# First product's right operand loaded in place of its low part; four more pairs begun early; last sums delayed

## The chip, the cores and the metric

The kernel runs on one core of a Trainium2 chip. The metric is device time of one execution in microseconds, the median over runs. Five engines run their own instruction queues in order: PE (TensorE) multiplies, DVE (VectorE) and ACT (ScalarE) do elementwise work and bring results out of PSUM, POOL (GpSimd) does a few small operations and issues some DMAs, SP (SyncE) issues most DMAs. An instruction that waits for a semaphore holds all behind it in its queue.

## The reference

One layer of a hybrid encoder over x of 2048 rows by 1024 columns, in float32:

```
y = rmsnorm(x); z = y @ w_in                 # 1024 x 2576
a = gmlp_mixer(zu, zv, ...)                  # spatial gating in blocks of 128 rows
b = gla_mixer(zq, zk, zv, zg, zlr, ...)      # gated linear attention, chunks of 64 rows
m = concat([a, b]) @ w_out
h = x + rmsnorm(m)
f = rmsnorm(h) @ w_ff1                       # 1024 x 4096
f = square(relu(f)) @ w_ff2                  # 4096 x 1024
out = h + rmsnorm(f)
```

Every float32 operand of a large product is split into a high part (rounded to the fast format) and a low part (the rest), and three products of parts are added (`mm3`, L143).

## The kernel before

The mixer works on four blocks of 512 rows (b = 0 to 3). For each it forms the columns of z in groups (`group`, L579): vb, q, k, g, then the previous block's out-projection (`out_proj`, L541), then v and u. Smaller work (attention, gating, norms, transposes) is put between the matmuls by a list of jobs, `Jobs`, one step or more after each of the eight k steps of a product. In this part PE's order is the written one, and a scheduler orders DVE, ACT, POOL and SP.

The first product of the feed-forward, f = rmsnorm(h) @ w_ff1, is done in two halves of 1024 rows (p = 0, 1) and 16 column groups (q), by Strassen's scheme in Winograd's form: seven block products p1 to p7, of which each takes one left operand (a block or sum of w1 blocks) and one right operand (a block or a sum of blocks of the transposed, normalised h). Step s is the pair (p, q), so steps 0 to 15 are the first half, 16 to 31 the second. One block product is one tick: 12 matmuls of 512 columns. The order of ticks is `seq` (L651): within a step p2, p6, p5, p7, then p1 of the next step, p4, p3. Products of chain A (p1, p6, p7, p4) add up in one PSUM bank, which ACT copies out in between: p7 may start only when p6 has been copied, p4 only when p7 has. Work on the other engines hangs on ticks by a table, `plan`, and after L648 the order of all engines is the written one.

The right operand has seven keys (`RIGHT`: b11, b21, t2, t1, t3, t4, b22) of four k each: 28 pairs of a high and a low tile of 128 x 512 for each half, numbered n = 0 to 27. Blocks come from `ht_d` in HBM, the transposed h; the sums t1 to t4 come from `b_d`, which `sums` (L499) fills for the first half during the last block's first groups: it reads blocks of `ht_d` into two tiles `hs`, takes four differences on DVE, and stores them. To make a pair, `read_ht` loads 256 KB into a staging tile `hr`, `split_ht` copies it to the high tile on ACT (the rounding) and subtracts the high tile from the staging tile on DVE, into the low one. For p = 0 `ahead` (L627) does this for 20 pairs during the last out-projection, with four staging tiles of tag "four"; pairs 20 to 27 are staged in the first four ticks, in tiles of the weights' staging tag. For p = 1 `ht_in` (L748) stages a pair in tiles of tags "four", "hts" or "w2s" one to three keys ahead of its tick in step 15, and `ht_split` makes it two ticks after the key's last use by step 15. The tags "four" and "w2s" also carry the second product's right operand on its way to HBM (`split_w2`, `read_w2`; tiles th, tl, w2s and the tensor t_d). High and low tiles take the 36 buffers of tag "big" that the mixer used, and for n = 10 to 19 the 20 buffers of the pool `fr`.

The second product runs after the first, with the right operand read back from t_d. In names of tiles in the profile hh and hl are the high and low part of the right operand, wh and wl of a weight or left operand, ws a weight's staging tile, abh and abl the parts of the mixer's output, zu, zvb the groups' outputs, u, ux, uy the results of a step, pp a group's or the out-projection's PSUM bank, pf the first product's.

Of the kernel before, what the change touches and what calls it, by code (L numbers as in the profile page):

```python
# [9 lines left out]
F32 = mybir.dt.float32  # L10
# [3 lines left out]
ALU = mybir.AluOpType  # L14
# [3 lines left out]
P = 128  # L18
D = 1024
# [11 lines left out]
NQ = 16  # L31
RP = 1024
NP = S // RP
H = RP // 2
# [9 lines left out]
FIRST = ("p1", "p2", "p6", "p5", "p7", "p4", "p3")  # L44
# [58 lines left out]
def trunk(  # L103
# [4 lines left out]
    v, a, pe, pool, dma = nc.vector, nc.scalar, nc.tensor, nc.gpsimd, nc.sync  # L108
# [5 lines left out]
    wp = ctx.enter_context(tc.tile_pool(name="wp", bufs=1, reuse_waits="tile"))  # L114
# [9 lines left out]
    ht_d = [dram.tile([P, KT, TB], F32, name=f"ht_d{b}") for b in range(NB)]  # L124
    f_d = [[dram.tile([P, 2, D], F32, name=f"f_d{p}_{q}") for q in range(NQ)] for p in range(NP)]
    b_d = [[dram.tile([P, 4, H], F32, name=f"b_d{p}_{k}") for k in range(4)] for p in range(NP)]
# [10 lines left out]
    def slot(name, dt=F32, tag="big"):  # L137
        return big.tile([P, 512], dt, name=name, tag=tag, bufs=4 if tag == "four" else NBIG)

    def split_lo(out_lo, src, hi):  # L140
        v.tensor_tensor(out_lo, src, hi.bitcast(F32), ALU.subtract)  # L141
# [9 lines left out]
    def rsqrt(small, ss, n, scale, name):  # L151
        r = small.tile([P, n], F32, name=f"rs_{name}", tag="rs", bufs=9)
        v.tensor_scalar(r, ss, scale, EPS, ALU.mult, ALU.add)
        pool.tensor_tensor(r, r, mhalf[:, :n], ALU.pow)
        return r
# [35 lines left out]
    def stage(name):  # L191
        return wp.tile([P, 512], F32, name=name, tag="ws", bufs=NS)
# [301 lines left out]
        eng.tensor_tensor(out_, x_, y_, ALU.add)  # L494

    def minus(eng, out_, x_, y_):
        eng.tensor_tensor(out_, x_, y_, ALU.subtract)

    def sums(p, k):  # L499


        bs_ = []
        for c in range(2):
            st = wp.tile([P, D], F32, name=f"hs{p}_{k}_{c}", tag="xr", bufs=4)
            for n in range(2):
                dma.dma_start(st[:, n * H:(n + 1) * H], ht_d[2 * p + n][:, k + 4 * c, :])
            bs_.append((st[:, 0:H], st[:, H:RP]))
        (b11, b12), (b21, b22) = bs_
        t1, t2 = (wp.tile([P, 512], F32, name=f"ht{n}_{p}_{k}", tag="hts", bufs=2) for n in (1, 2))
        yield 1  # L510
        minus(v, t1, b12, b11)
        minus(v, t2, b22, t1)
        minus(v, b12, b22, b12)
        minus(v, b21, b21, t2)
        for n, t in enumerate((t1, t2, b12, b21)):
            dma.dma_start(b_d[p][k][:, n, :], t)

    ht = {}
    PAIRS = [(key, k) for key in RIGHT for k in range(4)]

    def read_ht(p, n, st):

        key, k = PAIRS[n]
        if key[0] == "t":
            dma.dma_start(st, b_d[p][k][:, int(key[1]) - 1, :])
        else:
            dma.dma_start(st, ht_d[2 * p + int(key[2]) - 1][:, k + 4 * (int(key[1]) - 1), :])

    def split_ht(p, n, st):
        key, k = PAIRS[n]  # L530
        pair = []
        for part in "hl":
            if 10 <= n < 20:
                pair.append(fr.tile([P, H], F32R, name=f"h{part}{p}_{key}_{k}", tag="ht", bufs=20))
            else:
                pair.append(slot(f"h{part}{p}_{key}_{k}", F32R))
        hi, lo = ht[p, key, k] = pair
        a.copy(hi, st)
        split_lo(lo, st, hi)

    def out_proj(b, steps=2, also=None):  # L541
        def before(hf, k):
# [40 lines left out]
    for b in range(NB):  # L583
# [10 lines left out]
        if b == NB - 1:  # L594
            jobs.add(*((lambda k=k: sums(0, k), 1) for k in range(4)))
# [26 lines left out]
        finish(b, 3)  # L622
        jobs.add(*((lambda i=i: gate(i), 4) for i in tiles))
    fr = br = None
    begun_ht = []

    def ahead(hf, k):  # L627

        nonlocal fr, br
        if hf == 0 and k == 1:  # L630
            mixp.close()
            br = ctx.enter_context(tc.tile_pool(name="br", bufs=1, side="right", reuse_waits="tile"))
            fr = frp.enter_context(tc.tile_pool(name="fr", bufs=1, side="right", reuse_waits="tile"))
        for _ in range(2 if hf or k == 3 else int(1 <= k < 3)):
            if len(begun_ht) < 20:
                n = len(begun_ht)
                st = slot(f"hr0_{n}", tag="four")
                read_ht(0, n, st)
                split_ht(0, n, st)
                begun_ht.append(n)  # L640

    out_proj(NB - 1, 4, ahead)


# [9 lines left out]
    at = {sn: i for i, sn in enumerate(seq)}  # L654
    todo = {}

    def plan(tick, fn, *args):
        todo.setdefault(tick, []).append((fn, args))

    def do(tick):  # L660
        for fn, args in todo.pop(tick, ()):
            fn(*args)
# [54 lines left out]
    def norm_m():  # L717
        v.tensor_tensor(sh[:, 0, :], sh[:, 0, :], sh[:, 1, :], ALU.add)
        last_h["r"] = rsqrt(wp, sh[:, 0, :], TPB, 1.0 / D, "m_last")

    def residual(t):
        h, xr = last_h[t]
        v.scalar_tensor_tensor(h, h, last_h["r"][:, t:t + 1], xr, ALU.mult, ALU.add)
        dma.dma_start(h_d[NT - TPB + t], h)
        a.activation(xr, h, AF.Square, accum_out=sh[:, 2, t:t + 1])
# [17 lines left out]
        plan(tick, fn, *args)  # L743


    staged = {}

    def ht_in(p, n):  # L748
        if p == 0:
            st = stage(f"hr{p}_{n}")  # L750
        elif n % 12 < 4:
            st = slot(f"hr{p}_{n}", tag="four")
        elif n % 12 < 6:
            st = wp.tile([P, 512], F32, name=f"hr{p}_{n}", tag="hts", bufs=2)
        else:
            if n % 2 == 0:
                staged["two"] = br.tile([P, D], F32, name=f"hr{p}_{n}", tag="w2s", bufs=3)
            st = staged["two"][:, n % 2 * H:(n % 2 + 1) * H]
        staged[p, n] = st
        read_ht(p, n, st)  # L760

    def ht_split(p, n):
        split_ht(p, n, staged.pop((p, n)))

    for n in range(20, 28):
        plan((n - 20) // 2, ht_in, 0, n)
        plan((n - 20) // 2 + 1, ht_split, 0, n)
    for n in range(28):

        plan(at[NQ - 1, FIRST[n // 4 - 3]] + 2 if n >= 12 else at[NQ - 1, "p1"] + 1 + n // 8, ht_in, 1, n)  # L770
    for n in range(28):
        todo.setdefault(at[NQ - 1, FIRST[n // 4]] + 2, []).insert(n % 4, (ht_split, (1, n)))


    def sums_in(k):
# [218 lines left out]
        read_w1(1, n)  # L994
    for i in sorted(j for j in todo if j < 0):
        do(i)
    norm_m()
    residual(0)
    for i in range(len(seq)):
# [120 lines left out]
    for m, (p, c) in enumerate(chunks):  # L1120
        banks = {}
        final = m == NCH - 1
        for grp in ((0, 1), (2, 3)) if final else (range(NPAIR),):
            for n7, n in enumerate(SECOND):
                name, key, chain = WINO[n]
                j = 7 * m + n7
                if grp[0] == 0 and j + 2 < 7 * NCH:
                    read_t(j + 2)
                for r in grp:
# [4 lines left out]
                    for kk in range(2):  # L1134
                        hi, lo = left[m, name, kk]
# [83 lines left out]
```

## Time and profile before

| | |
|---|---|
| runs | 2060.32, 2061.06, 2061.36 us; median 2061.06 |
| profiled execution | 2057.67 us, of which its span is 2055.7 |
| PE busy | 1999.5 us (97%), 9504 matmuls |
| DVE busy | 1422.9 us (69%) |
| ACT busy | 979.5 us (48%) |
| DMA | 446.86 MB, mean 217 GB/s |
| mean granted clock of TensorE | 0.992 |

The profile is of one execution. "Idle before" is the time that an engine sat idle ahead of an instruction, with what released it. The granted clock is the share of TensorE's 2.4 GHz that it was given. The last out-projection runs from about 734 to 782 us, the first product from 782 to about 1420 us, and its change from the first to the second half of the rows lies around 1080 to 1125 us.

### The profile page before, as it was taken

How to read it: one execution, taken by the hardware profiler on the slowest of the kernel's cores; microseconds unless marked ns; L12 is line 12 of the kernel's file. 1: busy time of each engine (PE TensorE's matmuls, PEld its weight loads, DVE VectorE, ACT ScalarE, POOL GpSimd, SP SyncE). 2: the span in 40 equal slices, each digit the busy share in tenths (PEclk: the TensorE clock that was granted, in tenths of full speed). 3: DMA queues.
4: the chain of work that ended last, by engine and by line, in shares of the span. 5: the costliest groups of instructions: out<-in, count | busy, mean ns of one | idle time of the engine just before them, and what ended most of it. 6: DMA issues, size and time to landing. Idle time of an engine off the chain costs nothing.

```text
span 2055.7 us, 27515 instructions
## 1 busy us (share of the span) xinstructions
PE 1999.5 (97%) x9504; PEld 1654.6 (80%) x9504; DVE 1422.9 (69%) x2491; ACT 979.5 (48%) x1942; POOL 250.7 (12%) x410
## 2 busy tenths in 40 slices
PE   8999999999899998999998999999999999999996
PEld 6989887988788886888887788888888888788885
DVE  4474467356735775657677677775888888988877
ACT  5464465356344555556667666666221214222212
POOL 0010011002100200003321333231000002100011
PEclk9999999999999999999999999999999999999998
DMA  7434245424852554758888878888767677866674
GB/s 217 126 114 132 81 141 149 148 78 154 260 177 86 166 197 144 249 197 259 287 288 287 274 276 289 285 273 292 265 236 264 237 265 272 323 253 257 242 268 185
DMA packets 165212, 446.86 MB, mean 217 GB/s; under 512 B 23488, under 2 KB 48592, under 8 KB 151376
## 3 DMA queue, kind: packets, MB, share of 16 engines
q1 hardware_dynamic: 138464, 355.42, 51.7%
q0 software_dynamic: 26608, 89.67, 12.3%
q8 instruction: 75, 1.23, 0.2%
q14 instruction: 65, 0.53, 0.1%
HBM read 319.19 MB, written 125.83 MB: 216 GB/s over the span
## 4 chain that ended last, share of the span: by engine, by line
PE 75%; DMA 9%; DVE 6%; issue 4%; ACT 3%; POOL 2%; SPq 0%; POOLq 0%; DVEq 0%; ACTq 0%
PE po_A L144 5%; PE po_A L145 5%; PE po_A L146 5%; PE pf_A L144 5%; PE pf_A L146 5%; PE pf_A L145 4%; PE pp_o L144 3%; PE pp_o L146 3%; PE pp_o L145 3%; PE po_C L144 2%; PE po_C L145 2%; PE po_C L146 2%; PE pf_C L144 2%; PE pf_C L146 2%; PE pf_C L145 2%
## 5 line engine op out<-in xcount | busy, mean ns | idle before, releaser
L494 DVE TENSOR_TENSOR acc<-acc,po_A 128x512 f32<-128x512 f32 x232 | 159.3, 687 | 47.3 <-PE po_A L146 33.0
L950 ACT CAST sh_s<-r 128x512 fp32r<-128x512 f32 x96 | 55.6, 618 | 165.4 <-PE po_A L146 92.9
L950 ACT CAST sh_a<-f 128x512 fp32r<-128x512 f32 x94 | 54.6, 618 | 130.4 <-DMA f<-f_d 92.6
L144 PE MATMUL pf_A<-hl_t,wh_s 128*128 128x512 f32 x256 | 102.5, 400 | 10.6 <-ACT uy L895 6.9
L141 DVE TENSOR_TENSOR wl_s<-s,wh_s 128x512 fp32r<-128x512 f32 x96 | 66.1, 689 | 60.6 <-ACT wh_s L692 60.5
L144 PE MATMUL pp_o<-wl_o,abh 128*128 128x512 f32 x256 | 103.8, 406 | 2.3 <-DVE h L451 2.0
L144 PE MATMUL po_A<-tt,sh_s 128*128 128x512 f32 x256 | 100.7, 393 | 2.5 <-DVE acc L494 1.4
L219 DVE SCALAR_TENSOR_TENSOR wl_o<-ws_o,outg,wh_o 128x512 fp32r<-128x512 f32 x64 | 47.9, 749 | 78.7 <-ACT wh_o L218 78.5
L146 PE MATMUL pf_A<-hh_t,wl_s 128*128 128x512 f32 x256 | 101.4, 396 | 0.0
L145 PE MATMUL pf_A<-hh_t,wh_s 128*128 128x512 f32 x256 | 100.8, 394 | 0.0
L144 PE MATMUL po_C<-tt,sh_s 128*128 128x512 f32 x256 | 100.5, 392 | 0.3 <-DMA tt<-t_d_b 0.3
L146 PE MATMUL pp_o<-wh_o,abl 128*128 128x512 f32 x256 | 100.4, 392 | 0.0
L145 PE MATMUL pp_o<-wh_o,abh 128*128 128x512 f32 x256 | 100.4, 392 | 0.0
L145 PE MATMUL po_A<-tt,sh_s 128*128 128x512 f32 x256 | 100.3, 392 | 0.0
L145 PE MATMUL po_C<-tt,sh_s 128*128 128x512 f32 x256 | 100.2, 392 | 0.0
L146 PE MATMUL po_A<-tt,sl_s 128*128 128x512 f32 x256 | 99.9, 390 | 0.0
L146 PE MATMUL po_C<-tt,sl_s 128*128 128x512 f32 x256 | 99.9, 390 | 0.0
L144 PE MATMUL po_A<-tt,sh_a 128*128 128x512 f32 x248 | 97.5, 393 | 0.5 <-DMA tt<-t_d_t 0.5
L494 DVE TENSOR_TENSOR acc<-acc,po_C 128x512 f32<-128x512 f32 x120 | 82.5, 687 | 21.4 <-PE po_C L146 14.0
L145 PE MATMUL po_A<-tt,sh_a 128*128 128x512 f32 x248 | 97.1, 392 | 0.0
L146 PE MATMUL po_A<-tt,sl_a 128*128 128x512 f32 x248 | 96.8, 390 | 0.0
L141 DVE TENSOR_TENSOR wl_a<-w1s,wh_a 128x512 fp32r<-128x512 f32 x96 | 66.0, 687 | 41.9 <-ACT wh_a L692 41.9
(299 smaller groups left out, 5974.1 us busy)
## 6 DMA issues: line engine op xcount, KB each, us to landing
tt<-t_d_t SPq DMA_DIRECT2D x61, 1024.0 KB, 6.0
tt<-t_d_b SPq DMA_DIRECT2D x46, 1024.0 KB, 4.8
w1s<-in_w SPq DMA_DIRECT2D x64, 512.0 KB, 5.1
f<-f_d SPq DMA_DIRECT2D x64, 512.0 KB, 7.1
ws_o<-in_w_out SPq DMA_DIRECT2D x64, 256.0 KB, 2.6
w2s<-in_w POOLq DMA_DIRECT2D x32, 512.0 KB, 6.4
t_d_t<-th_t POOLq DMA_DIRECT2D x64, 256.0 KB, 5.0
t_d_t<-tl_t POOLq DMA_DIRECT2D x64, 256.0 KB, 4.7
```

Source lines behind the costliest of these rows:

```text
L141: v.tensor_tensor(out_lo, src, hi.bitcast(F32), ALU.subtract)
L144: pe.matmul(ps, ahi, blo, start=start, stop=False, **kw)
L145: pe.matmul(ps, ahi, bhi, start=False, stop=False, **kw)
L146: pe.matmul(ps, alo, bhi, start=False, stop=stop, **kw)
L219: v.scalar_tensor_tensor(lo, st, gain, hi.bitcast(F32), ALU.mult, ALU.subtract)
L494: eng.tensor_tensor(out_, x_, y_, ALU.add)
L950: a.copy(hi, src)
```

## The change

Three edits. First, `read_ht` now takes both tiles of a pair and loads the values straight into the low one; `split_ht` copies from there to the high tile and subtracts in place. No staging tile is left, and `ht_in`, `ht_split` and their staging go. For p = 1 a key is read right behind its last tick in step 15 and split three ticks later (before: staged earlier, split two ticks later). Second, `ahead` reads by a table and splits a call later what was read the call before; it reads 24 pairs (before: 20) in the out-projection. The last four are read before the first tick and split at ticks 2 and 3. Third, `sums` yields 5 in place of 1 between its reads and its differences, takes its two DVE tiles only then, and the first difference keeps its place in the written order. PE's and POOL's instructions stand in the same order as before.

```
     def sums(p, k):
...
         (b11, b12), (b21, b22) = bs_
+        yield 5
         t1, t2 = (wp.tile([P, 512], F32, name=f"ht{n}_{p}_{k}", tag="hts", bufs=2) for n in (1, 2))
-        yield 1
-        minus(v, t1, b12, b11)
+        tc.keep_in_program_order(minus(v, t1, b12, b11))
...
-    def read_ht(p, n, st):
...
-            dma.dma_start(st, b_d[p][k][:, int(key[1]) - 1, :])
-        else:
-            dma.dma_start(st, ht_d[2 * p + int(key[2]) - 1][:, k + 4 * (int(key[1]) - 1), :])
-
-    def split_ht(p, n, st):
+    def read_ht(p, n):
         key, k = PAIRS[n]
         pair = []
         for part in "hl":
...
-        hi, lo = ht[p, key, k] = pair
-        a.copy(hi, st)
-        split_lo(lo, st, hi)
+        ht[p, key, k] = pair
+        if key[0] == "t":
+            dma.dma_start(pair[1].bitcast(F32), b_d[p][k][:, int(key[1]) - 1, :])
+        else:
+            dma.dma_start(pair[1].bitcast(F32), ht_d[2 * p + int(key[2]) - 1][:, k + 4 * (int(key[1]) - 1), :])
+
+    def split_ht(p, n):
+        hi, lo = ht[(p,) + PAIRS[n]]
+        a.copy(hi, lo.bitcast(F32))
+        split_lo(lo, lo.bitcast(F32), hi)
...
     def ahead(hf, k):
...
-        for _ in range(2 if hf or k == 3 else int(1 <= k < 3)):
-            if len(begun_ht) < 20:
...
+        if hf == 0:
+            n = {1: 3, 2: 6, 3: 9}.get(k, 0)
+        else:
+            n = {4: 12, 5: 14, 6: 16, 7: 18, 0: 20, 1: 22, 2: 23, 3: 24}[k]
+        for j in range(begun_ht[1], begun_ht[0]):
+            split_ht(0, j)
+        begun_ht[1] = begun_ht[0]
+        for j in range(begun_ht[0], n):
+            read_ht(0, j)
+        begun_ht[0] = max(n, begun_ht[0])
...
+    for n in range(24, 28):
+        plan(n // 2 - 10, split_ht, 0, n)
+    for n in range(28):
+        plan(at[NQ - 1, FIRST[n // 4]], read_ht, 1, n)
+        todo.setdefault(at[NQ - 1, FIRST[n // 4]] + 3, []).insert(n % 4, (split_ht, (1, n)))
...
-    for n in range(20, 28):
-        plan((n - 20) // 2, ht_in, 0, n)
-        plan((n - 20) // 2 + 1, ht_split, 0, n)
-    for n in range(28):
-        plan(at[NQ - 1, FIRST[n // 4 - 3]] + 2 if n >= 12 else at[NQ - 1, "p1"] + 1 + n // 8, ht_in, 1, n)
-    for n in range(28):
-        todo.setdefault(at[NQ - 1, FIRST[n // 4]] + 2, []).insert(n % 4, (ht_split, (1, n)))
...
+    for n in range(begun_ht[1], 24):
+        split_ht(0, n)
+    for n in range(24, 28):
+        read_ht(0, n)
     norm_m()
```

SP's queue in the last block, where q's weights (ws_3_q) are loaded. b_d0 is the store of a difference, hs0 a read for the sums. Before:

```order
L516 DMA b_d0_1_130<-ht1_0_1_5930 128x512
L208 DMA ws_3_q_0_6008<-in_w_in 128x256
L516 DMA b_d0_1_130<-ht2_0_1_5931 128x512
L516 DMA b_d0_1_130<-hs0_1_0_5924 128x512
L516 DMA b_d0_1_130<-hs0_1_1_5927 128x512
L516 DMA b_d0_2_131<-ht1_0_2_5964 128x512
L208 DMA ws_3_q_0_6008<-in_w_in 128x16
L506 DMA hs0_3_0_6000<-ht_d0_93 128x512
L516 DMA b_d0_2_131<-ht2_0_2_5965 128x512
L516 DMA b_d0_2_131<-hs0_2_0_5958 128x512
L516 DMA b_d0_2_131<-hs0_2_1_5961 128x512
L506 DMA hs0_3_0_6000<-ht_d1_94 128x512
```

After, around the first store of a difference:

```order
L208 DMA ws_3_q_4_6054<-in_w_in 128x256
L208 DMA ws_3_q_4_6054<-in_w_in 128x16
L208 DMA ws_3_q_5_6073<-in_w_in 128x256
L208 DMA ws_3_q_5_6073<-in_w_in 128x16
L208 DMA ws_3_q_6_6092<-in_w_in 128x256
L208 DMA ws_3_q_6_6092<-in_w_in 128x16
L516 DMA b_d0_0_129<-ht1_0_0_6000 128x512
L516 DMA b_d0_0_129<-ht2_0_0_6001 128x512
L516 DMA b_d0_0_129<-hs0_0_0_5890 128x512
L516 DMA b_d0_0_129<-hs0_0_1_5893 128x512
```

The stores and reads of the sums stood among the first two weights of q; now they begin behind the seventh.

ACT's queue in the last out-projection, up to the first eviction of its first half (h12 from pp_o3_0_0). wh_o3 is a weight, hr0 a staged read. Before:

```order
L218 ACTIVATE wh_o3_1_7_8050<-ws_o3_1_7_8048,outg_198 128x512
L538 CAST hh0_b21_3_7984<-hr0_7_7982 128x512
L538 CAST hh0_t2_0_8008<-hr0_8_8006 128x512
L218 ACTIVATE wh_o3_1_0_8080<-ws_o3_1_0_8078,outg_198 128x512
L538 CAST hh0_t2_1_8014<-hr0_9_8012 128x512
L450 ACTIVATE h12_7929,ssm3_7930<-pp_o3_0_0_7692 128x512
```

After:

```order
L218 ACTIVATE wh_o3_1_7_8064<-ws_o3_1_7_8062,outg_198 128x512
L539 CAST hh0_t1_3_8031<-hl0_t1_3_8032 128x512
L539 CAST hh0_b11_3_7884<-hl0_b11_3_7885 128x512
L218 ACTIVATE wh_o3_1_0_8092<-ws_o3_1_0_8090,outg_198 128x512
L539 CAST hh0_b21_0_7887<-hl0_b21_0_7888 128x512
L539 CAST hh0_b21_1_7890<-hl0_b21_1_7891 128x512
L450 ACTIVATE h12_7944,ssm3_7945<-pp_o3_0_0_7692 128x512
```

The casts just ahead of the evictions were of b21's last pair and of the first two pairs of t2, and are now of t1, b11 and the first two of b21. Earlier in this queue two casts of t2 now stand ahead of weight wh_o3_1_4 and two of t1 around the last cast abh15, where no cast of the right operand stood before.

ACT's queue where the second half's right operand begins (hh1), in step 15. wh_15 and wh_16 are left operands, uy14, ux15 and uy15 results of steps, and the COPY takes p6 of step 15 out of its bank. Before:

```order
L692 CAST wh_15_s1_10892<-s1_15_10790 128x512
L538 CAST hh1_b11_0_10924<-hr1_0_10896 128x512
L538 CAST hh1_b11_1_10928<-hr1_1_10898 128x512
L538 CAST hh1_b11_2_10932<-hr1_2_10900 128x512
L538 CAST hh1_b11_3_10936<-hr1_3_10902 128x512
L692 CAST wh_15_s3_10940<-w1s15_1_10643 128x512
L857 ACTIVATE uy14_10687<-uy14_10687 128x512
L858 ACTIVATE uy14_10687<-uy14_10687 128x512
L692 CAST wh_16_a11_10977<-w1s16_0_10739 128x512
L857 ACTIVATE ux15_10863<-ux15_10863 128x512
L858 ACTIVATE ux15_10863<-ux15_10863 128x512
L895 COPY uy15_10864<-pf15_A_10850 128x512
```

After:

```order
L697 CAST wh_15_s1_10876<-s1_15_10762 128x512
L697 CAST wh_15_s3_10893<-w1s15_1_10615 128x512
L841 ACTIVATE uy14_10659<-uy14_10659 128x512
L842 ACTIVATE uy14_10659<-uy14_10659 128x512
L539 CAST hh1_b11_0_10843<-hl1_b11_0_10844 128x512
L539 CAST hh1_b11_1_10846<-hl1_b11_1_10847 128x512
L539 CAST hh1_b11_2_10849<-hl1_b11_2_10850 128x512
L539 CAST hh1_b11_3_10852<-hl1_b11_3_10853 128x512
L697 CAST wh_16_a11_10924<-w1s16_0_10711 128x512
L841 ACTIVATE ux15_10835<-ux15_10835 128x512
L842 ACTIVATE ux15_10835<-ux15_10835 128x512
L879 COPY uy15_10836<-pf15_A_10822 128x512
```

The four casts of b11 stood ahead of the squares of uy14; now they stand behind them, still ahead of the squares of ux15 and the copy.

## Rows read from the trace of the kernel before

**Rows 1.** The page's first part: span, TensorE.

```profile
span 2055.7 us, 27515 instructions
...
PE 1999.5 (97%) x9504; PEld 1654.6 (80%) x9504; DVE 1422.9 (69%) x2491; ACT 979.5 (48%) x1942; POOL 250.7 (12%) x410
```

**Rows 2.** Busy time by stretch: instructions in brackets, granted clock, DMA share, GB/s.

```profile
core 0: us, PE busy (x) PEld busy (x) DVE busy (x) ACT busy (x) POOL busy (x), PEclk, DMA share, GB/s
740.00:830.00 90.00, 81.66 (x358) 65.81 (x357) 58.86 (x92) 54.28 (x100) 2.41 (x3) 0.94 0.57 185
1080.00:1165.00 85.00, 77.99 (x332) 62.83 (x331) 63.35 (x103) 60.93 (x111) 16.19 (x30) 0.98 0.84 279
```

**Rows 3.** TensorE in order of time: start, length, idle before it, releaser.

```profile
540.67 0.50 PE L144 MATMUL pp_vb<-wl_vb,yh 128*128 128x512 f32 x1 [1.57 <-ACT zu L283]
...
566.31 0.39 PE L144 MATMUL pp_q<-wl_q,yh 128*128 128x272 f32 x1 [3.83 <-ACT zvb L283]
...
758.14 0.79 PE L144 MATMUL pp_o<-wl_o,abh 128*128 128x512 f32 x1 [2.05 <-DVE h L451]
...
797.86 0.50 PE L144 MATMUL pf_A<-hl_t,wh_s 128*128 128x512 f32 x1 [3.29 <-ACT u L895]
...
812.45 0.59 PE L144 MATMUL pf_C<-hl_b,wh_s 128*128 128x512 f32 x1 [2.26 <-DVE hl_b L141]
...
1096.72 0.51 PE L144 MATMUL pf_A<-hl_t,wh_s 128*128 128x512 f32 x1 [2.07 <-ACT uy L895]
...
1120.17 0.80 PE L144 MATMUL pf_A<-hl_t,wh_s 128*128 128x512 f32 x1 [3.60 <-ACT uy L895]
```

**Rows 4.** Stretches of the same length, behind a wait and later; columns as in rows 2.

```profile
758.10:761.50 3.40, 3.36 (x8) 2.68 (x9) 3.40 (x6) 2.47 (x7) 0.00 (x0) 0.50 0.63 234
762.00:765.40 3.40, 3.40 (x17) 2.78 (x16) 1.88 (x4) 1.75 (x3) 0.00 (x0) 1.00 0.49 132
```

**Rows 5.** SP's waits in 518 to 572 (total, times, longest), and ScalarE's timeline.

```profile
SPq L516 <- DVE ht L497: 9.5, 8, 2.2
...
563.67 0.42 ACT L215 CAST wh_q<-ws_q 128x272 fp32r<-128x272 f32 x1 [6.54 <-DMA ws_q<-in_w_in]
```

**Rows 6.** ScalarE's timeline: the square ahead of u's fourth eviction.

```profile
539.32 0.63 ACT L425 ACTIVATE zv<-zu 128x512 f32<-128x512 f32 x1 [1.47 <-DVE zu L423]
```

**Rows 7.** VectorE groups in 1040 to 1160, a difference written over its input.

```profile
L497 DVE TENSOR_TENSOR w1s<-w1s,w1s 128x512 f32<-128x512 f32 x6 | 4.1, 682 | 0.0
```

**Rows 8.** ScalarE's timeline around the last out-projection.

```profile
740.77 0.72 ACT L218 ACTIVATE wh_o<-ws_o,outg 128x512 fp32r<-128x512 f32 x1 [2.00 <-PE pp_o L146]
...
754.85 0.62 ACT L538 CAST hh_t<-hr 128x512 fp32r<-128x512 f32 x1 [1.43 <-DMA hr<-b_d]
...
794.93 1.20 ACT L538 CAST hh_t<-hr 128x512 fp32r<-128x512 f32 x2
...
811.06 1.26 ACT L538 CAST hh_b<-hr 128x512 fp32r<-128x512 f32 x2 [5.36 <-DMA hr<-ht_d]
```

**Rows 9.** Waits of SP (1055 to 1150) and ScalarE (1065 to 1150).

```profile
SPq L527 <- DMA t_d_t<-th_t: 8.0, 1, 8.0
...
ACT hh_b L538 <- DMA hr<-ht_d: 4.8, 4, 1.9
```

**Rows 10.** ScalarE's and VectorE's timelines in the change of row half.

```profile
1109.60 2.17 ACT L538 CAST hh_t<-hr 128x512 fp32r<-128x512 f32 x4
...
1110.24 2.49 DVE L141 TENSOR_TENSOR hl_t<-hr,hh_t 128x512 fp32r<-128x512 f32 x4
...
1114.57 0.63 ACT L857 ACTIVATE uy<-uy 128x512 f32<-128x512 f32 x1 [1.76 <-DVE uy L494]
```

**Rows 11.** DMA in 1078 to 1112 (40 slices); to landing of all reads of hr.

```profile
GB/s 400 130 0 67 299 255 5 260 287 169 304 215 217 130 214 328 152 304 313 287 349 289 328 362 398 328 253 318 417 405 446 400 405 417 390 402 395 386 388 390
...
hr<-b_d SPq DMA_DIRECT2D x16, 256.0 KB, 7.0
...
DMA to landing us min/median/max: 2.0/5.1/15.8
```

More of the change, by code (lines that the diff above doesn't have):

```diff
@@ L496, in minus @@
     def minus(eng, out_, x_, y_):
-        eng.tensor_tensor(out_, x_, y_, ALU.subtract)
+        return eng.tensor_tensor(out_, x_, y_, ALU.subtract)
     def sums(p, k):
@@ L519, in trunk @@
     PAIRS = [(key, k) for key in RIGHT for k in range(4)]
-    def read_ht(p, n, st):
-        key, k = PAIRS[n]
-        if key[0] == "t":
-            dma.dma_start(st, b_d[p][k][:, int(key[1]) - 1, :])
-        else:
-            dma.dma_start(st, ht_d[2 * p + int(key[2]) - 1][:, k + 4 * (int(key[1]) - 1), :])
-    def split_ht(p, n, st):
+    def read_ht(p, n):
         key, k = PAIRS[n]
@@ L624, in trunk @@
     fr = br = None
-    begun_ht = []
+    begun_ht = [0, 0]
     def ahead(hf, k):
@@ L633, in ahead @@
             fr = frp.enter_context(tc.tile_pool(name="fr", bufs=1, side="right", reuse_waits="tile"))
-        for _ in range(2 if hf or k == 3 else int(1 <= k < 3)):
-            if len(begun_ht) < 20:
[L636 to L640, printed above, removed]
+        if hf == 0:
[8 more added lines that the diff above has]
+        begun_ht[0] = max(n, begun_ht[0])
     out_proj(NB - 1, 4, ahead)
@@ L743, in trunk @@
         plan(tick, fn, *args)
-    staged = {}
[L748 to L763, printed above, removed]
-    for n in range(20, 28):
-        plan((n - 20) // 2, ht_in, 0, n)
-        plan((n - 20) // 2 + 1, ht_split, 0, n)
-    for n in range(28):
-        plan(at[NQ - 1, FIRST[n // 4 - 3]] + 2 if n >= 12 else at[NQ - 1, "p1"] + 1 + n // 8, ht_in, 1, n)
-    for n in range(28):
-        todo.setdefault(at[NQ - 1, FIRST[n // 4]] + 2, []).insert(n % 4, (ht_split, (1, n)))
+    for n in range(24, 28):
[3 more added lines that the diff above has]
+        todo.setdefault(at[NQ - 1, FIRST[n // 4]] + 3, []).insert(n % 4, (split_ht, (1, n)))
+    staged = {}
     def sums_in(k):
```

## The prediction

> **What bounds the kernel now.** I read the page's first part, the waits of TensorE in order of time, the queues behind each wait, and last the granted clock. TensorE is busy 1999.5 of 2055.7 us [rows 1], so it sets the time, and a change that leaves its matmuls alone, as this one does, can only move the 56 us in which it is idle and the stretches in which it runs slowly. Three stages hold much of that: PE is busy 81.66 of 90 us around the last out-projection and 77.99 of 85 us where the second half of the rows takes over [rows 2]; the third is the last block's vb and q groups. Their waits are seven [rows 3]: A, 1.57 before a vb matmul and 3.83 before q; B, 2.05 between the halves of the out-projection, 3.29 before (0, p7) and 2.26 before (0, p3); C, 2.07 and 3.60 before (15, p7) and (16, p7). Right behind five of them the granted clock is 0.50, the lower level (1.2 GHz), for about 3.4 us: the one behind 758.14 is shown, with 8 matmuls where the same length at full clock has 17 [rows 4]; the others stand behind 566.31, 797.86, 812.45 and 1120.17. Each costs half its length, 1.7 us. The 2.07 us wait at 1096.72 is followed by none. So the seven waits with their five slow stretches are 18.67 + 8.5 = 27.2 us, the most that this change can reach.
>
> **A: the delayed sums.** Before, q's weights wait in SP's queue behind stores of sums that DVE has not made yet: SP stood 9.5 us, eight times, for them, and ACT waited 6.54 us for a q weight with the eviction of vb behind it in its own queue [rows 5]. That eviction is what q waits for. In the new order seven q loads stand ahead of the first store. The three differences that came before the vb eviction on DVE are gone too; the square at 539.32, which had waited 1.47 us for DVE, stands ahead of the fourth eviction of u, which PE waits 1.57 us for [rows 6, 3]. I let both waits go, 1.57 + 3.83, with the slow stretch behind q, 1.7: **7.1 us**. What is late next: the sums now stand among the weights of q, k and g. Reading a buffer again waits for its store, and SP then holds the k weights. There are five staging buffers and six pairs of converted weights ahead of PE, so a hold of one store and one load hides; from below the gain is 0 (the wait moves to k), from above 7.1. I take 7.1, since the loads that PE needs first are all ahead.
>
> **B: reads into the low part, four more pairs early.** The 56 copies and 56 subtractions stay. Only the operand of the subtraction changes, to its own output, and the trace has such subtractions: 682 ns [rows 7], four in a row with a staged source 2.49 us [rows 10], so nothing is paid. What changes is who waits for a buffer. Before, a read waits for one of four staging buffers, and ACT, in order, waits for the read: 1.43 us just ahead of the evictions between the halves, and 5.36 us in the first ticks, with p3's operand [rows 8]. After, SP issues the reads as fast as PE and the mixer's pool leave buffers.
> Between the halves: wait 2.05, slow stretch 1.7. The casts ahead of the evictions are now of pairs whose reads SP issues without waiting for a staging buffer; a read lands after 2.0 to 15.8 us, median 5.1 [rows 11]. I leave 0.6 us of the wait and count 1.45 + 1.7 = **3.15**; bounds 0 and 3.75.
> Two casts now stand ahead of the out-projection's weight at 740.77, where ACT had been idle 2.00 us [rows 8], and two more near the last abh, which TensorE needs within 2 us. Two casts fit, their landing may not: cost **0.6**, bounds 0 and 3.1 (a median landing less that idle time).
> The wait of 3.29: ACT's chain of residual, square and scale stays, and only the two casts of 1.20 us at 794.93, ahead of the copy, go [rows 8]. **1.2**; the slow stretch stays (2.1 us of wait is left, and 2.05 was followed by one). Bounds 0 and 3.29 + 1.7.
> The wait of 2.26: its pairs are read at the end of the out-projection instead of two ticks before use, so it goes with its slow stretch: **3.96**, bounds 0 and 3.96.
> B is 3.15 - 0.6 + 1.2 + 3.96 = 7.7 us.
>
> **C: the second half's right operand.** The first wait comes from four staging buffers that were still being stored: SP stood 8.0 us for a store, the reads came late, and ACT idled 4.8 us for them with the copy of p6 behind [rows 9]. After, no staging buffer is needed, and the casts stand a tick later, behind the squares. The 2.07 goes. A read can start only when PE has used the low part for the last time, and is cast three ticks later, 8.5 us (seven ticks took 1120.17 - 3.60 - 1096.72 = 19.85 us [rows 3], 2.84 each); reads of sums landed after 7.0 us median there [rows 11]. That fits, barely.
> The second wait is work: between the copies of (15, p7) and (16, p6) ACT does 16 casts and 5 of weights at 0.54 (four in 2.17), four Relu and Square pairs at 1.26, and two copies, 0.5 each: 8.7 + 2.7 + 5.0 + 1.0 = 17.4 us [rows 10]. Without the first wait (15, p7) would start at 1094.65, its copy is due at 1097.5, and (16, p7) starts seven ticks later, at 1114.5: ACT is done at 1114.9, 0.4 late, and 1.76 more if it waits for DVE as it did [rows 10]. I allow 0.5 for the copy behind it. 5.67 becomes 2.7: **3.0**, and the slow stretch stays. Bounds: nothing (the wait goes to 5.67) and 5.67 + 1.7.
>
> **Sum.** 7.1 + 7.7 + 3.0 = 17.8 us. The profiled execution took 2057.67 us (its span and 2.0 around it), so it would take 2039.9; the median of the three runs stands 3.4 above it, and I forecast from that: 2061.06 - 17.8 = **2043.3**.
>
> **A rule that speaks against C.** In 1078 to 1112 the slices of DMA traffic run at 386 to 446 GB/s from 1102 on [rows 11]. The new order issues four groups of four reads in four successive ticks, 4.2 MB in 11.4 us, 370 GB/s, and weights and stores run beside them. The Trainium skill ("DMA: Bandwidth & Descriptors", Bandwidth) has HBM's share of one core bind at about 358 GB/s; by it these reads alone would take 11.7 us, an estimate, the later groups would land past their casts, and it would side with the slower rival below. The measured slices are above its figure, so I do not take it.
>
> **Rivals.**
> 1. The reads are late in the out-projection as well: ACT waits there as before and B gives nothing. For it: ACT is in order, and a landing can take 15.8 us [rows 11]. Against: SP issues the reads many places ahead. 2061.06 - 7.1 - 3.0 = 2051.0.
> 2. The sums only move the hold of SP to k or g: A gives nothing. For it: SP stood 9.5 us for them [rows 5], and the same stores are still in its queue. Against: more weights are ahead of them. 2061.06 - 10.7 = 2050.4. Both together with C at nothing are no change, 2061.
> 3. Slower: a read for the second half now lies between the last use of its buffer and its cast, where before it went to staging two groups earlier. If reads land later than 8.5 us, ACT waits in each of seven groups with the copies behind it, PE waits for ACT, and the next buffers come free later. Each us past 8.5 costs 7 us. A and B without C are 14.8, so it turns slower than before from 8.5 + 14.8 / 7 = 10.6 us; at 12 us it is 2061.06 - 14.8 + 24.5 = 2071. For it: 15.8 was seen, and 7.0 is the median of sums. Against: both are with eight and more reads at once, which the new order spreads.
> 4. All seven waits and slow stretches go: 2033.9. Against: C's ACT work alone does not fit.
>
> **Chances.** Forecast (10 to 25 us gained) 0.58, range 2036 to 2051; rival 4 or near it 0.05; rival 1 0.15; rival 2 0.07; no change 0.07; rival 3 0.08. About 0.2%, 4.1 us, can be told from no change. Faster 0.58 + 0.05 + 0.15 + 0.07 = 0.85, same 0.07, slower 0.08. The range reaches from rival 4 to beyond rivals 1 and 2: 2034 to 2056; what is left out is the two worse cases and a little at the fast end.
>
> **What would show it.** Right: no wait of PE before pp_q and pp_vb's fourth tile, ACT without a DMA wait ahead of the evictions at the middle of the out-projection, no wait before the first p3, one slow stretch there in place of three; in the second half's change-over no ACT wait for a read, and one PE wait of 2 to 3 us before (16, p7). Wrong: q's wait found again before pp_k or pp_g; ACT idle for reads of hl in the out-projection; casts of the second half that wait for DMA.

## The result, and the profile after

The changed kernel takes 2040.22 us (median of six runs, 2037.61 to 2044.24) where the kernel before takes 2060.31 (six runs beside it): a ratio of 0.9903, 95% interval 0.9891 to 0.9916. The forecast was 2043.3, with 2034 to 2056 as its range. The profiled execution's span is 2036.6 us.

The page's first part, as in [rows 1]: TensorE has the same 9504 matmuls and is busy 5.5 us less, mostly since three slow stretches, 1.7 us each, are gone.

```profile
span 2036.6 us, 27539 instructions
...
PE 1994.0 (98%) x9504; PEld 1651.4 (81%) x9504; DVE 1422.3 (70%) x2491; ACT 980.8 (48%) x1942; POOL 251.1 (12%) x410
```

Busy time over the same matmuls as in [rows 2] (columns as there). The first stretch is 6.6 us shorter than its 90, the second 5.2 shorter than its 85.

```profile
732.10:815.50 83.40, 78.71 (x359) 63.67 (x358) 58.75 (x93) 54.75 (x100) 2.41 (x3) 0.98 0.64 216
1065.30:1145.10 79.80, 77.26 (x332) 63.06 (x331) 63.09 (x103) 60.26 (x112) 16.32 (x31) 0.98 0.88 301
```

TensorE's waits from 520 to 1165 us (start, length, idle before it, releaser), to be held against [rows 3]. Nothing waits any more before pp_vb's fourth tile, pp_q, the first p3, (15, p7) and (18, p7), which had waited 1.23 us at 1161.48; the wait before abh's matmul and that before g are new.

```profile
583.63 0.50 PE L144 MATMUL pp_g<-wl_g,yh 128*128 128x512 f32 x1 [0.65 <-DVE zk L574]
...
740.24 0.50 PE L144 MATMUL pp_o<-wl_o,abh 128*128 128x512 f32 x1 [0.89 <-ACT abh L270]
750.82 0.50 PE L144 MATMUL pp_o<-wl_o,abh 128*128 128x512 f32 x1 [1.06 <-DVE h L451]
...
787.82 0.50 PE L144 MATMUL pf_A<-hl_t,wh_s 128*128 128x512 f32 x1 [2.17 <-ACT u L879]
1101.63 0.50 PE L144 MATMUL pf_A<-hl_t,wh_s 128*128 128x512 f32 x1 [2.54 <-ACT uy L879]
```

Two slow stretches are left of the five, behind the last two rows. The first of them beside 3.4 us behind 750.82, where the clock stayed at its upper level:

```profile
789.00:792.40 3.40, 3.40 (x11) 2.52 (x10) 2.53 (x6) 2.98 (x7) 0.00 (x0) 0.50 0.49 157
...
750.80:754.20 3.40, 3.38 (x15) 2.82 (x16) 3.15 (x6) 3.34 (x9) 0.00 (x0) 1.00 1.04 411
```

TensorE's instructions stand in one order in all kernels below, so a stage can be measured between the starts of the same two matmuls. Stages are named by the times of those matmuls in the profile of before; each entry is from one profiled execution, in us.

| kernel | A: 520-600 | B1: 735-784 | B2: 784-830 | C: 1078-1165 | median of runs |
|---|---|---|---|---|---|
| before | 79.90 | 48.99 | 46.07 | 86.98 | 2060.31 |
| changed | 72.47 | 47.97 | 40.28 | 81.78 | 2040.22 |
| changed again (g0) | 72.62 | 49.01 | 40.20 | 83.42 | 2043.72 |
| e1 sums only | 72.75 | 47.66 | 45.30 | 87.58 | 2053.68 |
| e2 twenty pairs | 72.98 | 47.90 | 47.96 | 81.76 | 2049.14 |
| e3 second half staged | 72.83 | 48.23 | 38.66 | 85.51 | 2047.94 |
| e4 split at 2 ticks | 73.49 | 48.61 | 40.18 | 85.37 | 2046.10 |
| e5 stores on POOL | 75.49 | 47.28 | 45.29 | 86.48 | 2054.94 |
| f1 square behind copy | 73.38 | 48.75 | 38.24 | 81.19 | 2041.52 |
| f3 casts behind evictions | 73.91 | 46.57 | 38.64 | 81.79 | 2039.67 |
| f6 three edits | 73.71 | 46.40 | 40.57 | 82.08 | 2040.35 |
| g1 best | 75.07 | 46.39 | 38.23 | 79.42 | 2036.70 |
| g2 casts behind copy | 73.93 | 48.83 | 38.64 | 84.87 | 2045.51 |

Of the 19.1 us between the two spans, A gave 7.4, B1 1.0, B2 5.8 and C 5.2; all other stages together took 0.3 back. No edit touches the stage from 6 to 300 us, and it took 291.99 us in e1 and 296.81 in f3, so a median alone can't place a gain of a few us. The stages can. (The experiments ran on three other chips, where the kernel before took 2061.26, 2061.53 and 2061.48.)

### The profile page after: what moved, and what is told of

It reads as the page before. It is cut to its first block, busy times and chain, and to the rows that moved or that the text cites. A ratio compares the mean times of both kernels' runs of the same rounds, so it can differ in the third digit from the quotient of the medians.

```text
span 2036.6 us, 27539 instructions
## 1 busy us (share of the span) xinstructions
PE 1994.0 (98%) x9504; PEld 1651.4 (81%) x9504; DVE 1422.3 (70%) x2491; ACT 980.8 (48%) x1942; POOL 251.1 (12%) x410
## 3 DMA queue, kind: packets, MB, share of 16 engines
q8 instruction: 75, 1.23, 0.2%
## 4 chain that ended last, share of the span: by engine, by line
PE 81%; DMA 6%; DVE 6%; ACT 3%; issue 2%; POOL 1%; SPq 0%; DVEq 0%; ACTq 0%; POOLq 0%
PE pf_A L144 6%; PE pf_A L146 6%; PE pf_A L145 6%; PE po_A L144 5%; PE po_A L145 5%; PE po_A L146 5%; PE pf_C L144 3%; PE pf_C L146 3%; PE pf_C L145 3%; PE pp_o L144 3%; PE po_C L144 2%; PE po_C L145 2%; PE po_C L146 2%; PE pp_o L146 2%; PE pp_o L145 2%
```

## The experiments

**Sums alone, on the kernel before (e1).** The edit is the third of the change: `yield 5`, the tiles behind it, and the first difference kept in its place.

> The kernel before with the delay of the sums alone. Theory (three parts that add up): the waits of TensorE in the last block's vb and q go (0.55 + 0.79 + 1.57 + 3.83 us) with the slow stretch behind q (1.7), and 0.65 comes back before g, so about 7.8 us below the kernel before: 2052.5. The waits of the out-projection and of the change of row half stay as they were. Rival: the gain in this place needs the reads of the other edit too (SP's hold only moves on), then it is 2058 to 2060.

Measured: 2053.68, ratio 0.997 (0.9955 to 0.9985), and A at 72.75, as in the changed kernel; B2 and C stay as before. TensorE (time, idle, releaser) in A and at the first p7, then SP's wait for differences (total, times, longest) in 518 to 600:

```profile
536.47 0.50 PE L144 MATMUL pp_vb<-wl_vb,yh 128*128 128x512 f32 x1 [0.49 <-ACT zu L283]
584.73 0.50 PE L144 MATMUL pp_g<-wl_g,yh 128*128 128x512 f32 x1 [0.36 <-DVE zk L573]
...
789.62 0.50 PE L144 MATMUL pf_A<-hl_t,wh_s 128*128 128x512 f32 x1 [3.21 <-ACT u L895]
```

```profile
SPq L516 <- DVE ht L497: 3.9, 6, 1.5
```

SP's 9.5 us of [rows 5] are 3.9, spread over the weights of q, k and g; the wait of 3.83 is gone and one of 0.36 stands before g. The gain of A belongs to the sums alone.

**Stores of the sums on POOL's queue, on the kernel before (e5).** VectorE's differences stay early.

```diff
-            dma.dma_start(b_d[p][k][:, n, :], t)
+            pool.dma_start(b_d[p][k][:, n, :], t)
```

> The kernel before with one edit: the 16 stores of the last block's sums are issued by POOL in place of SP; VectorE's differences stay at their early places. It tells apart what made q wait. Theory (SP's hold): the q weights no longer stand behind stores, ScalarE does not wait 6.5 us for one, and the wait of 3.83 us before q goes with its slow stretch; the waits of vb for u's evictions (0.79 and 1.57), which come from differences on VectorE, stay or halve. The stage from 520 to 600 us falls from 79.9 to 73.5 to 75, the run to 2054 to 2056. Rival (VectorE's order): the differences ahead of the evictions and of q's low parts are the cause, and the wait before q stays above 3 us; the stage stays at 79 to 80.

Measured: 2054.94, ratio 0.9969 (0.9957 to 0.9981), A at 75.49. TensorE in A:

```profile
542.79 0.50 PE L144 MATMUL pp_vb<-wl_vb,yh 128*128 128x512 f32 x1 [1.71 <-ACT zu L283]
568.49 0.39 PE L144 MATMUL pp_q<-wl_q,yh 128*128 128x272 f32 x1 [0.89 <-DVE wl_q L141]
```

So A had two causes. Stores in SP's queue made q wait: with them elsewhere 3.83 is 0.89, and ScalarE waits 0.3 us for a q weight's load in place of 6.54. Differences on VectorE made vb wait for u's eviction: with them in place 1.71 stays. The change takes both away.

**Twenty pairs begun, on the changed kernel (e2).**

```diff
-            n = {4: 12, 5: 14, 6: 16, 7: 18, 0: 20, 1: 22, 2: 23, 3: 24}[k]
+            n = {4: 12, 5: 14, 6: 16, 7: 18}.get(k, 20)
...
+    for n in range(20, 28):
+        plan((n - 20) // 2, read_ht, 0, n)
+        plan((n - 20) // 2 + 1, split_ht, 0, n)
```

> The changed kernel with 20 pairs begun in the out-projection in place of 24: pairs 20 to 27 are read in ticks 0 to 3, straight into their low tiles, and split one tick later. Theory: the last pairs are again read two ticks before p3, so ScalarE waits some 5 us for them and the wait of 2.26 us before the first p3 returns with its slow stretch: 4.0 us above the changed kernel, 2044. Rival: what made these reads late was the staging buffer and not the number of pairs, then there is no wait before p3 and the time is that of the changed kernel, 2040.

Measured: 2049.14; B2 is 47.96, 7.7 us above the changed kernel and not 4.0. ScalarE, then TensorE:

```profile
788.08 1.16 ACT L539 CAST hh_t<-hl_t 128x512 fp32r<-128x512 f32 x2
...
804.43 1.25 ACT L539 CAST hh_b<-hl_b 128x512 fp32r<-128x512 f32 x2 [6.89 <-DMA hl_b<-ht_d]
```

```profile
790.95 0.72 PE L144 MATMUL pf_A<-hl_t,wh_s 128*128 128x512 f32 x1 [3.24 <-ACT u L880]
...
805.83 0.50 PE L144 MATMUL pf_C<-hl_b,wh_s 128*128 128x512 f32 x1 [2.56 <-DVE hl_b L141]
...
814.87 1.93 PE L481 MATMUL ht<-ident,xq 128*128 128x128 f32 x8 [1.89 <-ACT xq L737]
```

Reading early is what counts: with the reads two ticks ahead ScalarE waits 6.89 us, though no staging is left. It costs at three places: two casts stand ahead of the copy of p6 again (3.24 for 2.17), p3 waits, and the scaled rows that follow in ScalarE's queue come late for TensorE's transposes. A slow stretch follows the first, as in the changed kernel, and the third. The theory's place and cause hold, its size was half of what was measured.

**Second half staged as before, on the changed kernel (e3).** `ht_in` and `ht_split` of before for p = 1.

```diff
-        plan(at[NQ - 1, FIRST[n // 4]], read_ht, 1, n)
-        todo.setdefault(at[NQ - 1, FIRST[n // 4]] + 3, []).insert(n % 4, (split_ht, (1, n)))
+        plan(at[NQ - 1, FIRST[n // 4 - 3]] + 2 if n >= 12 else at[NQ - 1, "p1"] + 1 + n // 8, ht_in, 1, n)
...
+        todo.setdefault(at[NQ - 1, FIRST[n // 4]] + 2, []).insert(n % 4, (ht_split, (1, n)))
```

> The changed kernel with the second half's right operand staged as before (own staging tiles, read one to three keys ahead, split two ticks after the last use). Theory: the waits before (15, p7) and (16, p7) are 2.07 and 3.60 us again in place of one of 2.54, and 1.23 at (18, p7) returns, 4.4 us in all: 2044.6. Rival: staging was not what made them late (SP's queue stands elsewhere now), then 2040 and one wait.

Measured: 2047.94; C is 85.51. TensorE's waits there, and ScalarE's for the staged reads in 1060 to 1115:

```profile
1085.68 0.50 PE L144 MATMUL pf_A<-hl_t,wh_s 128*128 128x512 f32 x1 [2.49 <-ACT uy L915]
1108.62 0.59 PE L144 MATMUL pf_A<-hl_t,wh_s 128*128 128x512 f32 x1 [3.52 <-ACT uy L915]
```

```profile
ACT hh_b L537 <- DMA hr<-ht_d: 5.2, 4, 1.8
```

Both waits are back, 3.7 us of C. That of (18, p7) isn't, and it comes and goes: g0 has it (1.38), the changed kernel's first profile not. The rest of the higher median is not in this stage: A, B1 and B2 are within 0.4 us of the changed kernel's or below, and most of the excess stands in stages that no edit touches (6 to 300 us: 295.17, there 293.93; 300 to 520: 222.17, there 219.50).

**Split two ticks behind the read, on the changed kernel (e4).** `+ 3` becomes `+ 2` for p = 1.

> The changed kernel with the second half's pairs split two ticks after their reads in place of three. Reads have 5.7 us to land, and their median from issue is 5.8. Theory: ScalarE now waits for reads in about half of the seven groups, 1 to 2 us each, with copies of p6 behind, and TensorE's wait grows from 2.54 to 5 or more in one or two places: 2043 to 2048. Rival: the landing has slack that the median hides, because the copies come late in their tick; then no read is waited for, and the time stays at 2040 or falls a little since fewer casts stand between (15, p7) and (16, p6).

Measured: 2046.10; C is 85.37. Of the 3.6 us above the changed kernel's first profile 1.4 are at (18, p7), where the wait comes and goes, and 2.2 are the edit's. ScalarE and TensorE:

```profile
1084.69 1.22 ACT L539 CAST hh_b<-hl_b 128x512 fp32r<-128x512 f32 x2 [2.31 <-DMA hl_b<-ht_d]
```

```profile
1107.85 0.50 PE L144 MATMUL pf_A<-hl_t,wh_s 128*128 128x512 f32 x1 [3.60 <-ACT uy L879]
```

Only b21's reads were waited for (3.2 us in all), not half of the groups. b21's reads need the third tick, and the others landed within two: the margin that the slower rival doubted is less than one tick, 2.84 us, for one key of seven.

**Squares behind the copy of p6, on the changed kernel (f1).**

```diff
         elif n == "p6":
             a.copy(u2, ps_)
+            squared(u1, u1)
...
-        if n == "p2":
-            squared(u1, u1)
```

> The changed kernel, with the Relu and Square of a step's first result put behind the copy of p6 in the next tick in ScalarE's order. Theory: the wait before (16, p7) is ScalarE's queue, since the two squares and their 1.58 us wait for VectorE stand ahead of a copy whose matmuls have long ended. Without them the copy is 2.8 us earlier and the wait of 2.54 goes with its slow stretch (the stage from 1078 to 1165, 81.8, falls to 77.5); the first p7's wait of 2.17 falls by 1.2. In all 5.5 to 7.5: 2033 to 2035. Rival: p6's own matmuls or the casts end the wait and the copy moves less than 1 us; then 2038 to 2041, and the later squares may hold casts of left operands, which would show as waits of TensorE for wl.

Measured: 2041.52, not 2033 to 2035. The first p7 waits 0.98 and B2 is 38.24, but most of that fall is the slow stretch that does not follow; where none follows in the changed kernel's order B2 is 38.64 to 38.66, so the edit gives 0.4. C falls only to 81.19: 4.4 us are gained at (16, p7) and 3.8 lost again at p4. TensorE at p4, then what stands in ScalarE's queue ahead of the copy that it waits for:

```profile
1108.68 0.50 PE L144 MATMUL pf_A<-hl_t,wh_a 128*128 128x512 f32 x1 [2.76 <-ACT uy L882]
```

```profile
1102.34 2.17 ACT L539 CAST hh_t<-hl_t 128x512 fp32r<-128x512 f32 x4
1104.41 0.62 ACT L697 CAST wh_a<-w1s 128x512 fp32r<-128x512 f32 x1
1104.93 2.18 ACT L539 CAST hh_b<-hl_b 128x512 fp32r<-128x512 f32 x4
```

The copy of p6 comes in time, and the wait stands before p4 for the copy of p7. Neither theory had this. ScalarE is busy 23.37 of 25.60 us here (1083.0 to 1108.6), and this edit of its order alone handed the wait on.

**Casts behind the evictions, on the changed kernel (f3).** `behind` holds ScalarE's last cast of abh, and later the last eviction of the half.

```diff
+        if (hf, k) != (0, 3) and begun_ht[0] > 0:
+            with tc.issue_after(behind[0]):
                 for j in range(begun_ht[1], begun_ht[0]):
                     split_ht(0, j)
```

> The changed kernel, with the casts of the right operand in the last out-projection queued on ScalarE behind the last cast of abh (first half) and behind the four evictions between the halves (second half). Theory: the waits that remain in that stage, 0.89 for abh and 1.06 for VectorE's h, come from those casts and their reads standing ahead; they go, and the stage from 735 to 784 falls from 48.0 to 46 or less. The casts have idle time behind the evictions. About 2 us: 2038. Rival: eight casts in one piece behind the evictions hold the weights of the second half or the first ticks' pairs; then a wait before a pp_o or the first pf matmuls takes the place of both, and the time is 2040 or more.

Measured: 2039.67, no clear gain over the changed kernel's 2040.22. B1 is 46.57, just short of the 46 that was expected; both waits are gone, and one of 0.90 stands before the first p1, as its rival has it.

**Both and a later residual (f6).** Besides f1 and f3, `(1, residual, 2)` becomes `(2, residual, 2)`.

> The changed kernel with both of these edits and a third: the residual and its square of the third row tile one tick later, behind the copy of p6 in the first step. Theory: the edits are in different stages and add up: 5.5 to 7.5 and 2 from the two, and the first p7's wait goes wholly (1 us more, with its slow stretch of 1.7 where that stood): 8 to 12 below the changed kernel, 2028 to 2032. Rival: the later residual delays the scaled rows that TensorE transposes at tick 9 and 10, or the slow stretches only move: 2034 or more.

Measured: 2040.35, the rival. B1 keeps f3's gain (46.40). The first p7 waits no more, but the rows scaled behind it do come late, with a slow stretch behind:

```profile
792.09 1.62 PE L482 MATMUL ht<-ident,xq 128*128 128x128 f32 x8 [2.46 <-ACT xq L740]
```

**The changed kernel again, the best version, and one more (g0, g1, g2)**, all on one chip. g1 is f1 and f3 with the second half's last three keys cast four ticks behind their reads; g2 is the changed kernel with t3 cast five and the last two keys four ticks behind.

```diff
-FIRST[n // 4]] + 3, []).insert
+FIRST[n // 4]] + (3 if n < 16 else 4), []).insert                  # g1
+FIRST[n // 4]] + (3, 3, 3, 3, 5, 4, 4)[n // 4], []).insert         # g2
```

> The changed kernel itself, on the chip of the two runs beside it, to tell the spread of stages that no edit touches. Theory: within 3 us of 2040, with the same four places of slow clock or one less; the stages 520 to 600, 735 to 784, 784 to 830 and 1078 to 1165 at 72.5, 48, 40.3 and 81.8. Rival: the gain of one of these stages depends on the run, and it is off by over 2 us.

> The changed kernel with the squares behind the copy of p6, with the out-projection's casts behind abh and the evictions, and with the second half's last three keys (t3, t4, b22) cast four ticks after their reads in place of three. Theory: at the change of row half ScalarE has more work than time, so the squares alone only moved the wait to p4's copy; with casts of three keys a tick later the copies of p6 and p7 come in time, and the waits of 2.54 and 2.76 both go. The stage 1078 to 1165 falls from 81.8 to 77.5 to 79, 735 to 784 to 46.5, 784 to 830 to 38.5: 2031 to 2035. Rival: the casts come too late for their first use, and TensorE waits for a low part of t3 or b22 instead; 2038 or more.

> The changed kernel with one edit: t3's casts five ticks after their reads, behind the copy of (16, p6), and those of t4 and b22 four. Theory (queue length): the copy comes 2.2 us earlier, the wait before (16, p7) falls from 2.54 to 0.3 to 0.6, with no slow clock behind it; t3's low parts are ready just in time. The stage 1078 to 1165 falls by 2.2 to 4: 2036 to 2038. Rival: the squares ahead of the copy wait for VectorE however short the queue, so the copy moves under 1 us; or t3 is late and (16, p7) waits for it: no gain.

Measured: g0 2043.72, ratio to before 0.9918 (0.9902 to 0.9934); g1 2036.70, ratio 0.9881 (0.9863 to 0.9899); g2 2045.51. g1 is faster than the kernel before and, on the same chip, than g0, though short of its 2031 to 2035: p4's wait is gone, and of the 2.54 us 1.52 stay, with no slow stretch behind either p7. Of the 7.0 us to g0 about 4.9 are the edits' (2.1 in B1, 0.4 in B2, 2.4 in C); the rest is in slow stretches and waits that also differ between profiles of one kernel. The 1.52 that stay stand behind a wait of ScalarE for VectorE, so ScalarE's own work is not all of it.

```profile
787.80 0.50 PE L144 MATMUL pf_A<-hl_t,wh_s 128*128 128x512 f32 x1 [0.99 <-ACT u L882]
...
1099.74 0.51 PE L144 MATMUL pf_A<-hl_t,wh_s 128*128 128x512 f32 x1 [1.52 <-ACT uy L882]
```

```profile
1095.33 0.63 ACT L844 ACTIVATE uy<-uy 128x512 f32<-128x512 f32 x1 [1.76 <-DVE uy L495]
```

In g2 the copy ends 0.6 us after TensorE went idle, about as its theory says, but t3's low part is later, the rival of its expectation. The rest of its high C is a wait of 2.20 at (18, p7) with a slow stretch, 4.1 us.

```profile
1102.41 0.50 PE L144 MATMUL pf_A<-hl_t,wh_s 128*128 128x512 f32 x1 [1.88 <-DVE hl_t L141]
```

g0 repeats A and B2 within 0.2 us, but B1 is 49.01 and C 83.42, and its median stands 3.7 above 2040, just outside what was expected.

## Why the prediction was right, and where not

**A, 7.1 forecast.** Measured 7.4 between the two profiles, and 4.8 to 7.4 when all that have the edit are held against the one profile of before (72.47 to 75.07). The step held: q's weights ahead of the stores, the differences out of the way, and 0.65 us of wait left before g. The two waits that it counts are gone in every profile with the edit; the spread comes from waits that it doesn't count, for u's weight, at an earlier tile of pp_vb and before g. The rival that SP's hold only moves to k or g fell with e1.

**B, between the halves: 3.15 less 0.6 forecast, and this step failed.** B1 fell by 1.0 us in the first pair of profiles, but the old form has 48.99, 47.66 (e1) and 47.28 (e5), mean 47.98, and the new form 47.97, 49.01, 47.90, 48.23, 48.61, 48.75 and 48.83, mean 48.47. No gain is shown; the means differ by 0.5 the other way, less than either form's spread. The prediction's own sign of being wrong, ScalarE idle for reads of hl in the out-projection, is in the changed kernel's profile (728 to 768 us):

```profile
ACT hh_t L539 <- DMA hl_t<-b_d: 5.1, 3, 2.6
```

What failed first is the wait, of which the prediction left 0.6 us: TensorE waited 1.06 to 2.83 us between the halves in the seven profiles of the new form (mean 1.7), and 1.90 to 2.29 in the three of the old (mean 2.1). That SP issues the reads "without waiting for a staging buffer" was true and not enough. The reads cast just ahead of the evictions stand in SP's queue behind the load of a weight, which waits 1.9 us for a buffer of its own, and then they have to land. In g0 (740 to 757 us) the first of the three reads at 745.91 landed 5.1 us after its issue, and the cast, evictions and TensorE behind it were late as in [rows 8] and [rows 3]:

```profile
SPq L208 <- DVE wl_o L219: 1.9, 1, 1.9
```

```profile
745.48 0.33 SPq L208 DMA_DIRECT2D ws_o<-in_w_out  x1
745.91 1.33 SPq L535 DMA_DIRECT2D hl_b<-ht_d  x3
```

```profile
751.08 0.62 ACT L539 CAST hh_b<-hl_b 128x512 fp32r<-128x512 f32 x1 [0.97 <-DMA hl_b<-ht_d]
```

```profile
754.97 0.50 PE L144 MATMUL pp_o<-wl_o,abh 128*128 128x512 f32 x1 [2.03 <-DVE h L451]
```

In the changed kernel's first profile that cast waited only 0.20, and TensorE 1.06. No run takes the weight's load out of the way, so how much of the wait it makes is open. A read into its final tile can also wait for a matmul that still reads the tile: SP stood 7.4 us for that in the changed kernel (735 to 760 us). But 7.1 of it begin at 752.9, when the evictions are over, and no matmul behind waits for those pairs.

```profile
SPq L533 <- PE pp_o L146: 7.4, 2, 7.1
```

Rival 1 is right for this place. The 0.6 for casts ahead of abh was too small: TensorE lost 0.6 to 2.0 us there in the seven profiles, mean 1.4 (the row of 0.89 delayed the matmuls behind it by 1.6). And the 1.7 for the slow stretch was a cost of one execution: neither e1 nor e5, with the same code there, has one behind a wait of 2.29 and 1.90. f3 shows what the stage can give, 1.9 us, and by what: not the reads but ScalarE's order.

**B, first p7 and p3: 1.2 + 3.96 forecast.** Measured 5.8, or 6.1 between the means of the old form (46.07, 45.30, 45.29) and the new (40.28, 40.20, 40.18, and 38.66, 38.64, 38.64 where no slow stretch follows p7). The wait of p7 is 2.17 where 2.1 was forecast. The other 4.7 us of the first pair are p3's, more than its 3.96; in e1, e5 and e2, where these pairs are read late too, TensorE's transposes behind p3 wait as well, 1.79, 1.96 and 1.89. By e2 the four pairs begun early do this, not the missing staging.

**C, 3.0 forecast.** Measured 5.2, and 3.6 in g0. The mechanism was right: the first wait is gone, and the second, called ScalarE's own work, is 2.54 where 2.7 was forecast, with its slow stretch. At these two places TensorE gained 2.37 and 0.95 us, 3.3 in all. The second wait stands on the same row as forecast, behind squares that wait for VectorE:

```profile
1099.81 0.63 ACT L841 ACTIVATE ux<-ux 128x512 f32<-128x512 f32 x1 [1.58 <-DVE ux L494]
...
1101.01 0.57 ACT L879 COPY uy<-pf_A 128x512 f32<-128x512 f32 x1
```

Of the other 1.9 us 1.5 are the wait of (18, p7), which the prediction does not count. It is not the change's: e5 lacks it in the old form, and g0, e4 and g2 have it in the new. Rival 3, reads that land too late, had the right mechanism and lost by its size: e4 takes one tick away, one key's reads come late, and 2.2 us are lost. The Trainium skill ("DMA: Bandwidth & Descriptors", Bandwidth) would have HBM's share of one core, about 358 GB/s, bind here. The trace does not bear that out: in the changed kernel (1060 to 1110 us, 40 slices) loads and stores together ran at up to 419 GB/s, and the median landing of these reads was 5.9 and 5.8 us, which three ticks hold.

```profile
GB/s 26 193 403 256 257 198 326 415 282 184 262 328 416 419 400 311 405 418 400 413 410 395 387 382 385 338 400 233 21 252 375 164 300 419 419 161 0 79 324 226
...
hl_t<-b_d SPq DMA_DIRECT2D x16, 256.0 KB, 5.9
hl_b<-ht_d SPq DMA_DIRECT2D x12, 256.0 KB, 5.8
```

**The sum** came out right partly by luck: 17.8 was forecast and 19.1 measured in the first pair of profiles (20.1 between the medians), with B1 1.5 too high and C 2.2 too low. The 1.0 of B1 and 1.5 of C's 5.2 are differences that other profiles of the same two forms do not repeat. On another chip the gain was 17.8 (2061.48 less 2043.72).

## What to carry to other kernels

A load straight into its final tile does away with the staging wait, but it still stands in its queue behind loads that wait for other buffers, still has to land, and may wait for whoever still reads the tile; look at all three before counting the gain. Where an engine is busy nearly all of a few ticks, a new order may only move the wait to the next copy in the chain, as in f1; it got shorter in g1, where casts were moved out of those ticks as well. Before a stall of one profile is priced, look whether the same code has it in a second one.

## What was not expected of the hardware

A wait costs more than its idle row: the one of 0.89 us at 740.24 delayed the matmuls behind it by 1.6, the one of 1.23 at 1161.48 by 1.5. And whether the granted clock falls to 0.50 behind a wait is not settled by the wait: the first p7 waited 2.16 or 2.17 us in six profiles (changed, g0, e3, e4, f3, g2), and a slow stretch followed in three (B2 40.2 to 40.3) and not in the other three (38.6 to 38.7). What decides it is not shown. It is 1.6 us that one profile can't promise.
